# Scores of an HGRN2 head for both directions in one call: wide products first, then 24 narrow ones on four column groups

## The chip, the cores and the metric

The kernel runs on one core of one Trainium2 chip. The metric is the device time of one execution in microseconds. Three runs of the kernel before gave 887.88, 888.44 and 889.48 us; the median, 888.44, is the time before.

## What is computed

The reference runs two blocks of a network over 256 latent tokens (and 256 context tokens) of width 1024. The change is in the first block's mixer, a gated linear recurrence with 8 heads (HGRN2), done in both directions and in chunks of 64 tokens:

```python
b = jnp.cumsum(logf, axis=3)                      # within a chunk of 64
qe = q * jnp.exp(b - b_ref); ke = k * jnp.exp(b_ref - b)
scores = jnp.where(mask, jnp.einsum('bhnik,bhnjk->bhnij', qe, ke), 0.0)
o_intra = jnp.einsum('bhnij,bhnjv->bhniv', scores, v)
...
o_inter = jnp.einsum('bhnik,bhnkv->bhniv', q * jnp.exp(b), s_start)
```

For each head and direction the outputs are masked scores times values, plus the queries times the state at the chunk's start. The results of the two directions are added, normalized per head, multiplied by a gate and multiplied by an output matrix. Ahead of all this stands a modulation (shift, scale and gate vectors of a product with `w_ada`), whose parts are summed over partitions by small products.

## The kernel before, in words

All weights are streamed: SyncE loads halves of a chunk (128 x 1024) into a ring of eight raw buffers, ScalarE makes the high part (`hi`, line 154) and VectorE the low part (`lo`, line 155) of each, and a projection multiplies in three products per k tile (lines 355 to 357: high by high, high by low, low by high). The order of the work on each engine is the order in which the program is written; nothing is rescheduled.

The HGRN2 part takes the heads in four pairs p = 0 to 3. For each pair there are projections for the forget gates of the two directions (`ff`, `fb`), for `q` and for `v`; `gates(d)` (VectorE and ScalarE) makes the factors `qe`, `ke`, `Q`, `K` and `kc` of a direction. `hg_side` then gives the pair's small products as a list of steps:

- `T_(hh)`: transposes of `kc` (line 618), copied to `kcT` by ScalarE (line 620).
- `SC_(hh, d)`: the scores of one head and direction in one PSUM bank. In each of the two blocks of 128 tokens, the two chunks' diagonal parts are done with 32 stationary columns (lines 640 and 642, 64 and 32 moving tokens); then one 128x128 product between the blocks (line 645); then two products between the chunks of a block with 64 stationary columns (line 651). VectorE copies the diagonal parts under a mask into `sct` (line 657), ScalarE copies the rest (lines 659 and 664), and with the second direction VectorE adds the two directions into `scm` (line 662).
- `S_(hh)`: the state (line 626), read from `kcT`. `O_(hh)`: the output (line 684) and its normalization (lines 689 to 692). `OT_(hh)`: transposes of the result (line 698).

A float32 product is two passes in the trace, each with its own weight load: 64 calls of line 640 give 128 loads and 128 matmuls. All of these steps take banks from a ring of four, named `x`; a step waits until the readers of the bank's last use are done.

The steps of pairs 0 to 2 stand in the list `side`; `fm_product` and the second `fb` loop call `tick` after each four k tiles, which puts one or two steps into TensorE's queue. The steps of pair 3 have no projections of a next pair to go among, and go by the list `slots` among the four products of the output gate (`g`, p = 0 to 3), one slot after each four k tiles, twelve passes. `ada_flush` puts the two sums over partitions of a part of the modulation (`ada_rows`, lines 592 and 593; each takes one bank `x`) behind the gate product p = 1. After the gate products, `row_product` multiplies by the output matrix.

Of the kernel before, what the change touches and what calls it, by code (L numbers as in the profile page):

```python
# [9 lines left out]
F32 = mybir.dt.float32  # L10
# [6 lines left out]
D = 1024  # L17
# [33 lines left out]
def kernel(ctx: ExitStack, tc: tile.TileContext, a, out):  # L51
# [17 lines left out]
    # A chunk is one or two halves of up to 1024 columns. A half is loaded, then split exactly into two  # L69
    # float32r parts, hi + lo.  # L70
    halves, chunks = [], []

    def add(hs, kind="split"):
        """hs: per half (parts, k tiles, columns); a part is (view of the half's tile, source)."""
        first = len(halves)
        for parts, k, n in hs:
            halves.append((parts, k, n, kind))
            assert k * n <= 1024, (k, n)
        chunks.append((first, len(halves)))
        return len(chunks) - 1  # L80
# [19 lines left out]
    class SplitPool:  # L100
        """Buffers for the two parts of bufs halves, for the halves under limit."""
# [13 lines left out]
    def pump(limit, hold=False):  # L115
        """Issue the loads and the splits that have a free buffer, splits of halves under limit only."""
# [49 lines left out]
    def use(i, keep=None, ahead=None):  # L166
        """The k tiles of chunk i as a list of (hi, lo); chunks before it (or before keep) are done with."""
# [17 lines left out]
    def part_done(i):  # L185
        """The first half of chunk i is done with."""
# [137 lines left out]
    def rstd_of(ms, width=1, n=1):  # L324
        """(ms / n + eps) ^ -0.5; ms [128, width], or [128, 2] to be added."""
# [8 lines left out]
    def mean_sq(junk, x, ms):  # L334
        """ms = the part of the mean over D of x ^ 2 that x holds."""
# [44 lines left out]
    def fm_product(chunk, nk=KT, x=None, tag="x", ticks=0):  # L380
        """Two feature tiles of a product over lat tokens -> one bank [128, 2, T]."""
# [65 lines left out]
    # rstd of the tokens, then the same on every partition  # L447
# [44 lines left out]
    # products of the gates, with the sums (a), the features (s) and the next weights' splits among them  # L492
# [66 lines left out]
    def ada_step(parts=(3, 4, 2)):  # L559
        """One chunk of the rest of the modulation: sums over k on each partition, then over partitions."""  # L560
# [49 lines left out]
    def hg_side(p, el, vt):  # L610
# [20 lines left out]
        def SC_(hh, d):  # L631
            e = el[d]
            z = bank("x")
            zd = z[:, 0:256].rearrange("p (b t) -> p b t", b=2)
            ha, hb = (0, 32) if d == 0 else (32, 0)
            for b in range(2):
                for c in range(2):
                    o = hh * 256 + b * 128 + 64 * c
                    ra, rb = slice(64 * c + ha, 64 * c + ha + 32), slice(64 * c + hb, 64 * c + hb + 32)
                    t_.matmul(zd[ra, b, 64 * c:64 * c + 64], e["ke"][:, o + ha:o + ha + 32], e["qe"][:, o:o + 64],  # L640
                              start=True, stop=True)
                    t_.matmul(zd[rb, b, rb], e["ke"][:, o + hb:o + hb + 32], e["qe"][:, o + hb:o + hb + 32],
                              start=True, stop=True)
            b1, b2 = e["blk"]
            t_.matmul(z[:, 256:384], flat(e["K"][:, hh, b1, e["k"], :]), flat(e["Q"][:, hh, b2, e["c"], :]),
                      start=True, stop=True)
            rA = slice(0, 64) if d == 0 else slice(64, 128)
            cB = slice(64, 128) if d == 0 else slice(0, 64)
            zo = z[:, 384:512].rearrange("p (b t) -> p b t", b=2)
# [846 lines left out]
```

## Time and profile before

| | us |
|---|---|
| median of the runs (lowest, highest) | 888.44 (887.88, 889.48) |
| span of the profiled execution, first to last instruction | 886.7 |
| TensorE matmul busy | 863.0 (97%) |
| TensorE weight load busy | 781.0 (88%) |
| VectorE busy | 618.6 (70%) |
| ScalarE busy | 512.9 (58%) |

The profile is of one execution, and only its span is given; a run's time has in addition what lies around the span, and the median of the runs is 1.7 us above it. In a row of a timeline the first number is the start in us from the span's start, the second the length in us, then come engine, line, instruction, `out<-in` with shapes, and how many instructions are merged in the row. The length of a matmul's record holds its way through the array, so records overlap, and the pace of TensorE is read from start to start.

### The profile page before, as it was taken

What the parts mean: (1) busy time and instruction counts of PE and PEld (TensorE: products, weight loads), DVE (VectorE), ACT (ScalarE), POOL (GpSimd) and SP (SyncE); (2) the same over time, 40 slices, a digit from 0 to 9 for tenths busy, and PEclk for the clock granted to TensorE, in tenths of its full rate; (3) what the DMA queues carried; (4) which work ended last, traced back from release to release, by engine and by line L of the source; (5) the groups of instructions that cost most, each with busy time, mean ns of one, the idle gap of its engine ahead of it and who ended that gap; (6) DMA issues with size and microseconds to landing.
All of it is one profiled execution on the core that took longest, in us unless ns stands there. A gap on an engine that the chain in (4) does not pass through costs nothing.

```text
span 886.7 us, 15396 instructions
## 1 busy us (share of the span) xinstructions
PE 863.0 (97%) x6144; PEld 781.0 (88%) x6144; DVE 618.6 (70%) x955; ACT 512.9 (58%) x823; POOL 17.3 (2%) x27
## 2 busy tenths in 40 slices
PE   4999999999999999999999999999999999999997
PEld 2679897988978999999998799999999899999995
DVE  7876878776888778977767736766486587555532
ACT  6877575673857575655545745756463575444431
POOL 1000000000000000000000000000000000000000
PEclk9999999999999999999999999999999999999999
DMA  9984472733634458776764374445596087656401
GB/s 313 276 280 167 131 250 78 258 116 116 216 122 156 154 192 294 253 246 208 236 213 95 122 225 138 130 141 158 184 312 195 24 285 243 191 190 190 161 1 47
DMA packets 131967, 161.98 MB, mean 183 GB/s; under 512 B 14136, under 2 KB 114488, under 8 KB 131896
## 3 DMA queue, kind: packets, MB, share of 16 engines
q1 hardware_dynamic: 129728, 155.80, 55.0%
q10 hardware_dynamic: 2168, 5.20, 1.7%
q8 instruction: 48, 0.79, 0.3%
q14 instruction: 23, 0.19, 0.1%
HBM read 159.93 MB, written 1.05 MB: 182 GB/s over the span
## 4 chain that ended last, share of the span: by engine, by line
PE 91%; ACT 3%; DVE 3%; DMA 2%; issue 1%; POOL 0%; SPq 0%; POOLq 0%; DVEq 0%; ACTq 0%
PE m L355 17%; PE m L356 17%; PE m L357 17%; PE x L355 8%; PE x L357 8%; PE x L356 8%; PE x L684 2%; DMA xT<-in_xcT_dram 1%; PE m L345 1%; PE x L345 1%; PE m L346 1%; PE m L341 1%; PE x L626 1%; PE x L346 1%; DMA raw<-in_hg_w_in_dram 1%; PE x L341 1%
## 5 line engine op out<-in xcount | busy, mean ns | idle before, releaser
L155 DVE TENSOR_TENSOR lo<-raw,hi 128x1024 fp32r<-128x1024 f32 (+1 forms) x264 | 310.0, 1204 | 134.0 <-ACT hi L154 131.0
L154 ACT ACTIVATE hi<-raw 128x1024 fp32r<-128x1024 f32 (+1 forms) x264 | 265.7, 1038 | 121.1 <-PE x L356 51.0
L355 PE MATMUL m<-hTh,hi 128*128 128x256 f32 (+1 forms) x560 | 178.8, 319 | 0.6 <-ACT hTh L425 0.6
L356 PE MATMUL m<-hTl,hi 128*128 128x256 f32 (+1 forms) x560 | 171.7, 307 | 0.2 <-DVE hTl L432 0.2
L357 PE MATMUL m<-hTh,lo 128*128 128x256 f32 (+1 forms) x560 | 171.4, 306 | 0.0
L355 PE MATMUL x<-hTh,hi 128*128 128x256 f32 x592 | 166.2, 281 | 0.0
L356 PE MATMUL x<-hTl,hi 128*128 128x256 f32 x592 | 165.1, 279 | 0.0
L357 PE MATMUL x<-hTh,lo 128*128 128x256 f32 x592 | 165.1, 279 | 0.0
L355 PEld LDWEIGHTS m<-hTh,hi 128*128 128x128 f32 x560 | 105.8, 189 | 9.2 <-issue 2.9
L355 PEld LDWEIGHTS x<-hTh,hi 128*128 128x128 f32 x592 | 111.2, 188 | 1.0 <-ACT hi L154 0.2
L356 PEld LDWEIGHTS x<-hTl,hi 128*128 128x128 f32 x592 | 110.8, 187 | 1.0 <-issue 0.2
L357 PEld LDWEIGHTS x<-hTh,lo 128*128 128x128 f32 x592 | 111.2, 188 | 0.0
L356 PEld LDWEIGHTS m<-hTl,hi 128*128 128x128 f32 x560 | 105.8, 189 | 5.7 <-DVE hTl L432 0.8
L357 PEld LDWEIGHTS m<-hTh,lo 128*128 128x128 f32 x560 | 105.4, 188 | 5.8 <-DVE lo L155 0.4
L355 PE MATMUL m<-hi,ah 128*128 128x512 f32 x248 | 97.2, 392 | 0.0
L357 PE MATMUL m<-hi,al 128*128 128x512 f32 x248 | 96.8, 391 | 0.0
L356 PE MATMUL m<-lo,ah 128*128 128x512 f32 x248 | 96.5, 389 | 0.0
L357 PEld LDWEIGHTS m<-hi,al 128*128 128x128 f32 x248 | 46.5, 188 | 10.6 <-DVE al L1141 0.4
L356 PEld LDWEIGHTS m<-lo,ah 128*128 128x128 f32 x248 | 46.6, 188 | 8.9
L355 PEld LDWEIGHTS m<-hi,ah 128*128 128x128 f32 x248 | 46.6, 188 | 8.9 <-ACT ah L1137 0.2
L355 PE MATMUL m<-hi,hTh 128*128 128x256 f32 x128 | 36.2, 283 | 0.0
L575 DVE SCALAR_TENSOR_TENSOR vr<-raw,cs,vr 128x1024 f32<-128x1024 f32 x28 | 35.8, 1280 | 0.4
(302 smaller groups left out, 1267.4 us busy)
## 6 DMA issues: line engine op xcount, KB each, us to landing
raw<-in_ffn_w_up_dram SPq DMA_DIRECT2D x44, 512.0 KB, 5.7
raw<-in_w_in_dram SPq DMA_DIRECT2D x42, 512.0 KB, 3.6
raw<-in_hg_w_in_dram SPq DMA_DIRECT2D x36, 512.0 KB, 4.9
raw<-in_w_ada_dram SPq DMA_DIRECT2D x32, 512.0 KB, 4.9
raw<-in_w_up_dram SPq DMA_DIRECT2D x32, 512.0 KB, 4.7
raw<-in_w_down_dram SPq DMA_DIRECT2D x32, 512.0 KB, 3.6
raw<-in_ffn_w_down_dram SPq DMA_DIRECT2D x22, 512.0 KB, 4.5
raw<-in_w_ada_dram SPq DMA_DIRECT2D x32, 256.0 KB, 4.5
```

Source lines behind the costliest of these rows:

```text
L154: s_.activation(h[:, :w], r[:, :w], AF.Copy)
L155: held.append(lambda r=r, h=h, l=l, w=w: v_.tensor_tensor(l[:, :w], r[:, :w], h[:, :w].bitcast(F32), op=OP.subtract))
L341: t_.matmul(o, hTl[:, k, c], w[k][0], start=False, stop=k == KT - 1)
L345: t_.matmul(o, hTh[:, k, c], w[k][0], start=k == 0, stop=False)
L346: t_.matmul(o, hTh[:, k, c], w[k][1], start=False, stop=False)
L355: t_.matmul(o, wh, xh, start=start, stop=False)
L356: t_.matmul(o, wh, xl, start=False, stop=False)
L357: t_.matmul(o, wl, xh, start=False, stop=stop)
L575: v_.scalar_tensor_tensor(acc, w[kk][0], cs[:, k:k + 1], acc, op0=OP.mult, op1=OP.add)
L626: t_.matmul(z[:, d * 128:(d + 1) * 128], kcT[hh][:, (2 * d + j) * 128:(2 * d + j + 1) * 128], vt[:, j, hh * 128:(hh + 1) * 128], start=j = ...
L684: t_.matmul(z[:, b * 128:(b + 1) * 128], l, r, start=i == 0, stop=i == len(terms) - 1)
```

## The change

`SC_` is called once per head and does both directions in two banks. First come the two 128x128 products between the blocks. The products between chunks, with 64 stationary columns before, are split into two of 32. All 24 products with 32 columns are put on lists by the 32-column group (PSUM partitions 0, 32, 64, 96) they write, six per group, and issued in rounds over the four groups. Copies and sums come behind all of them. The list of steps keeps its length by two empty steps (`len`). For the last pair the slots are set anew: the scores of both heads stand in the last two slots of gate product 2, the states in the first two, the outputs one slot later than before. `ada_flush` stands behind gate product 2 instead of 1. Comments and docstrings removed elsewhere are left out here.

```diff
             St[hh] = wk.tile([128, 2, 128], F32, tag="St", name="St")
             s_.activation(flat(St[hh]), z[:, 0:256], AF.Copy)
 
-        def SC_(hh, d):
-            e = el[d]
-            z = bank("x")
-            zd = z[:, 0:256].rearrange("p (b t) -> p b t", b=2)
-            ha, hb = (0, 32) if d == 0 else (32, 0)
-            for b in range(2):
+        def SC_(hh):
+
+
+
+            zs, groups = [], [[] for _ in range(4)]
+            for d in range(2):
+                e = el[d]
+                z = bank("x")
+                zs.append(z)
+                b1, b2 = e["blk"]
+                t_.matmul(z[:, 256:384], flat(e["K"][:, hh, b1, e["k"], :]), flat(e["Q"][:, hh, b2, e["c"], :]),
+                          start=True, stop=True)
+                zd = z[:, 0:256].rearrange("p (b t) -> p b t", b=2)
+                zo = z[:, 384:512].rearrange("p (b t) -> p b t", b=2)
+                ha, hb = (0, 32) if d == 0 else (32, 0)
+                for b in range(2):
+                    for i in range(2):
+                        g = 2 * d + i
+                        groups[g].append((zo[32 * g:32 * g + 32, b, :], e["K"][:, hh, b, e["sA"], 32 * i:32 * i + 32],
+                                          e["Q"][:, hh, b, e["sB"], :]))
+                    for c in range(2):
+                        o = hh * 256 + b * 128 + 64 * c
+                        ga, gb_ = 2 * c + ha // 32, 2 * c + hb // 32
+                        rb = slice(32 * gb_, 32 * gb_ + 32)
+                        groups[ga].append((zd[32 * ga:32 * ga + 32, b, 64 * c:64 * c + 64],
+                                           e["ke"][:, o + ha:o + ha + 32], e["qe"][:, o:o + 64]))
+                        groups[gb_].append((zd[rb, b, rb], e["ke"][:, o + hb:o + hb + 32],
+                                            e["qe"][:, o + hb:o + hb + 32]))
+            for n in range(max(len(g) for g in groups)):
+                for g in groups:
+                    if n < len(g):
+                        t_.matmul(*g[n], start=True, stop=True)
+            for d in range(2):
+                z, sc = zs[d], sc_t[d, hh]
+                zd = z[:, 0:256].rearrange("p (b t) -> p b t", b=2)
+                zo = z[:, 384:512].rearrange("p (b t) -> p b t", b=2)
+                ha, hb = (0, 32) if d == 0 else (32, 0)
+                rA = slice(0, 64) if d == 0 else slice(64, 128)
+                cB = slice(64, 128) if d == 0 else slice(0, 64)
                 for c in range(2):
-                    o = hh * 256 + b * 128 + 64 * c
-                    ra, rb = slice(64 * c + ha, 64 * c + ha + 32), slice(64 * c + hb, 64 * c + hb + 32)
-                    t_.matmul(zd[ra, b, 64 * c:64 * c + 64], e["ke"][:, o + ha:o + ha + 32], e["qe"][:, o:o + 64],
-                              start=True, stop=True)
-                    t_.matmul(zd[rb, b, rb], e["ke"][:, o + hb:o + hb + 32], e["qe"][:, o + hb:o + hb + 32],
-                              start=True, stop=True)
-            b1, b2 = e["blk"]
-            t_.matmul(z[:, 256:384], flat(e["K"][:, hh, b1, e["k"], :]), flat(e["Q"][:, hh, b2, e["c"], :]),
-                      start=True, stop=True)
-            rA = slice(0, 64) if d == 0 else slice(64, 128)
-            cB = slice(64, 128) if d == 0 else slice(0, 64)
-            zo = z[:, 384:512].rearrange("p (b t) -> p b t", b=2)
-            for b in range(2):
-                t_.matmul(zo[rA, b, :], e["K"][:, hh, b, e["sA"], :], e["Q"][:, hh, b, e["sB"], :],
-                          start=True, stop=True)
-            sc = sc_t[d, hh]
-            for c in range(2):
-                for r, q_ in ((slice(64 * c, 64 * c + 64), hb), (slice(64 * c + ha, 64 * c + ha + 32), ha)):
-                    i = slice(64 * c + q_, 64 * c + q_ + 32)
-                    v_.copy_predicated(sc[r, :, i], hmask[r, d:d + 1, i].to_broadcast([r.stop - r.start, 2, 32]),
-                                       zd[r, :, i])
-            s_.activation(sc[rA, :, cB], zo[rA], AF.Copy)
-            if True and d:
-                scm[hh] = wk.tile([128, 2, 128], F32, tag="scm", name="scm", bufs=2)
-                v_.tensor_add(scm[hh], sc_t[0, hh], sc)
-            xS[hh, d] = wk.tile([128, 128], F32, tag="xs", name="xs", bufs=4)
-            s_.activation(xS[hh, d], z[:, 256:384], AF.Copy)
+                    for r, q_ in ((slice(64 * c, 64 * c + 64), hb), (slice(64 * c + ha, 64 * c + ha + 32), ha)):
+                        i = slice(64 * c + q_, 64 * c + q_ + 32)
+                        v_.copy_predicated(sc[r, :, i], hmask[r, d:d + 1, i].to_broadcast([r.stop - r.start, 2, 32]),
+                                           zd[r, :, i])
+                s_.activation(sc[rA, :, cB], zo[rA], AF.Copy)
+                xS[hh, d] = wk.tile([128, 128], F32, tag="xs", name="xs", bufs=4)
+                s_.activation(xS[hh, d], z[:, 256:384], AF.Copy)
+            scm[hh] = wk.tile([128, 2, 128], F32, tag="scm", name="scm", bufs=2)
+            v_.tensor_add(scm[hh], sc_t[0, hh], sc_t[1, hh])
 
         def O_(hh):
             z = bank("x")
...
                     b1, b2 = e["blk"]
                     ql = flat(e["Q"][:, hh, b, e["c"], :]) if b == b1 else e["q2"][:, hh, :]
                     terms.append((ql, St[hh][:, d, :]))
-                    if hh in scm:
-                        if d:
-                            terms.append((scm[hh][:, b, :], vt[:, 2 + b, hc]))
-                    else:
-                        terms.append((sc_t[d, hh][:, b, :], vt[:, 2 + b, hc]))
+                    if d:
+                        terms.append((scm[hh][:, b, :], vt[:, 2 + b, hc]))
                     if b == b2:
                         terms.append((xS[hh, d], vt[:, 2 + b1, hc]))
                 for i, (l, r) in enumerate(terms):
...
                 t_.transpose(z[:, b * 128:(b + 1) * 128], on[hh][:, b * 128:(b + 1) * 128], ident)
             s_.activation(oT[p][:, hh, :], z[:, 0:256], AF.Identity, scale=vec("gn"))
 
-        order = [(T_, 0), (T_, 1), (SC_, 0, 0), (SC_, 0, 1), (SC_, 1, 0), (SC_, 1, 1), (S_, 0), (S_, 1),
-                 (O_, 0), (O_, 1)]
+        order = [(T_, 0), (T_, 1), (SC_, 0), (len, ()), (SC_, 1), (len, ()), (S_, 0), (S_, 1), (O_, 0), (O_, 1)]
         late = [(OT_, 0), (OT_, 1)]
         return tuple([lambda f=f: f[0](*f[1:]) for f in x] for x in (order, late))
 
...
-    T0, T1, SC00, SC01, SC10, SC11, S0, S1, O0, O1 = work
+    T0, T1, SC0, _, SC1, _, S0, S1, O0, O1 = work
     OT0, OT1 = late
-    slots = [[], [[T0], [T1], [], [SC00]], [[S0], [SC10, S1], [SC01], [SC11]], [[O0], [O1], [], [OT0]]]
+    slots = [[], [[T0], [T1], [], []], [[S0], [S1], [SC0], [SC1]], [[], [O0], [O1], [OT0]]]
...
-        if p == 1:
+        if p == 2:
             ada_flush()
```

## Rows read from the trace of the kernel before

**Rows 1.** The head of the profile page: span, then busy us, share and instructions.
```profile
span 886.7 us, 15396 instructions
PE 863.0 (97%) x6144; PEld 781.0 (88%) x6144; DVE 618.6 (70%) x955; ACT 512.9 (58%) x823; POOL 17.3 (2%) x27
```

**Rows 2.** What TensorE waited for, whole span: us in total, times, longest.
```profile
PE x L466 <- DVE sq L456: 11.8, 1, 11.8
PE x L592 <- ACT kcT L620: 1.8, 1, 1.8
PE x L345 <- DVE hTh L989: 1.0, 2, 0.8
```

**Rows 3.** Stretches: us, busy of PE, PEld, DVE, ACT, POOL, granted clock, DMA.
```profile
250.62:254.60 3.98, 3.98 (x14) 2.95 (x15) 3.98 (x6) 1.38 (x2) 0.00 (x0) 0.57 0.32 115
...
96.00:130.00 34.00, 34.00 (x315) 31.16 (x314) 26.49 (x52) 20.18 (x40) 1.40 (x2) 1.00 0.67 218
```

**Rows 4.** Timeline of TensorE around the two score calls of head 0.
```profile
96.25 0.39 PE L356 MATMUL m<-hTl,hi 128*128 128x512 f32 x1
96.47 0.40 PE L357 MATMUL m<-hTh,lo 128*128 128x512 f32 x1
96.80 0.24 PE L640 MATMUL x<-qe,ke 128*32 128x64 f32 x1
96.81 0.22 PE L642 MATMUL x<-qe,ke 128*32 128x32 f32 x1
...
96.88 0.22 PE L640 MATMUL x<-qe,ke 128*32 128x64 f32 x1
...
96.94 0.22 PE L640 MATMUL x<-qe,ke 128*32 128x64 f32 x1
96.94 0.20 PE L642 MATMUL x<-qe,ke 128*32 128x32 f32 x1
...
97.16 0.49 PE L645 MATMUL x<-Q,K 128*128 128x128 f32 x2
...
99.10 0.50 PE L355 MATMUL m<-hTh,hi 128*128 128x512 f32 x1
```

**Rows 5.** Timeline of TensorE, output products of head 0.
```profile
110.43 0.39 PE L684 MATMUL x<-St,Q 128*128 128x128 f32 x2
110.65 0.39 PE L684 MATMUL x<-St,q 128*128 128x128 f32 x2
```

**Rows 6.** Timeline of VectorE: last factor of pair 0, and idle time before splits.
```profile
96.70 0.41 DVE L829 TENSOR_TENSOR K<-K,b 128x256 f32<-128x256 f32 x1
...
111.06 2.36 DVE L155 TENSOR_TENSOR lo<-raw,hi 128x1024 fp32r<-128x1024 f32 x2 [1.06 <-ACT hi L154]
...
215.60 2.36 DVE L155 TENSOR_TENSOR lo<-raw,hi 128x1024 fp32r<-128x1024 f32 x2 [2.30 <-ACT hi L154]
```

**Rows 7.** Timeline of TensorE around the end of gate product 1.
```profile
246.36 0.28 PE L357 MATMUL m<-hTh,lo 128*128 128x256 f32 x1
...
247.72 1.12 PE L592 MATMUL x<-vr,ones 128*128 128x512 f32 x2
250.62 1.88 PE L592 MATMUL x<-vr,ones 128*128 128x512 f32 x2 [1.78 <-ACT kcT L620]
...
254.60 1.06 PE L626 MATMUL x<-vt,kcT 128*128 128x128 f32 x8
```

**Rows 8.** Timelines of ScalarE and VectorE in the same stretch.
```profile
249.98 1.08 ACT L620 ACTIVATE kcT<-x 128x512 f32<-128x512 f32 x2
...
250.88 1.22 DVE L155 TENSOR_TENSOR lo<-raw,hi 128x1024 fp32r<-128x1024 f32 x1
```

**Rows 9.** Timelines of TensorE and VectorE, head 7's output to the last transposes.
```profile
270.98 0.36 PE L355 MATMUL m<-hTh,hi 128*128 128x256 f32 x1
...
272.96 0.61 DVE L692 TENSOR_SCALAR on<-x,r 128x128 f32<-128x128 f32 x2 [0.88 <-POOL r L322]
273.89 0.60 PE L698 MATMUL x<-ident,on 128*128 128x128 f32 x4
```

## Prediction

> **What bounds the kernel now.** I read the head of the profile page first: TensorE is busy for 863.0 of 886.7 us [rows 1]. Busy records of matmuls overlap, so the next view is the list of what TensorE waited for. There, 11.8 us at the very start and 1.8 us on line 592 are the only waits above 1 us [rows 2]. The table of stretches then shows that in the HGRN2 part VectorE is busy for 26.49 of 34 us and ScalarE for 20.18, while DMA moves at 0.67 of its share [rows 3]. So TensorE's queue is the path, and an edit is worth the TensorE time it takes away, as long as VectorE, at three quarters of the time, can follow. The last view is the timeline of TensorE around one pair of score calls [rows 4], around the last pair of heads [rows 7] and at the end of the gate products [rows 9].
>
> **The scores of pairs 0 to 2 (six heads).** Each float32 product is two passes. In one head, TensorE goes from the last pass of a projection (96.47) to the next projection's first pass (99.10). A projection pass is followed by the next after 0.22 to 0.23 us (96.25 to 96.47), so the score work proper starts at 96.70 and takes 2.40 us. It is two calls, each with three kinds of stationary width: 32, 128, 64. At each change of width nothing is in flight for a moment: from 96.47 the 0.23 of the pass itself would end at 96.70, and the first 32-column pass starts at 96.80. That is 0.10 us per change. The 32-column part of one call lasts from 96.80 to the first 128-column pass at 97.16, 0.36 us [rows 4].
>
> The new call, step by step. First two 128x128 products, one for each direction: four passes at 0.11 us (two passes from 110.43 to 110.65 [rows 5]), 0.44 us; they have the width of the projection before them, so no change is paid there. Then one change, 0.10. Then 24 products with 32 columns, 48 passes, 12 on each 32-column group: eight of 64 tokens and four of 32. The 64-token passes of one group follow each other at about 0.06 us (96.88 to 96.94). The 32-token passes of two groups, eight of them, start between 96.81 and 96.94, at a pitch of about 0.04 within a group. That these start between the starts of the 64-token ones shows that the four groups run side by side. So a group needs 8 x 0.06 + 4 x 0.04 = 0.64 us. Behind the last pass comes what the old part shows behind its own four 64-token passes, 0.36 - 4 x 0.06 = 0.12. Sum: 0.44 + 0.10 + 0.64 + 0.12 = 1.30 us instead of 2.40, a gain of 1.10 per head. Bounds for the 0.64: at best a group never waits at all and its 32-token passes take half of a 64-token one (0.60); if the rounds of four march in step, 12 x 0.06 = 0.72; with no overlap of groups at all, 32 x 0.06 + 16 x 0.04 = 2.56.
>
> Of these heads, the first has a new wait. Its call now needs both directions' factors at once. The last write to K for the second direction ends on VectorE at 96.70 + 0.41 = 97.11 [rows 6]; the second 128x128 product would start at 96.70 + 0.22 = 96.92. That costs 0.2 us once. In the other pairs, the same factor is ready before the call. Six heads: 6 x 1.10 - 0.2 = 6.4 us.
>
> Queues behind this: the mask copies and ScalarE's copies keep their number and their order by direction; the sum of the two directions comes as before behind both. The second bank is asked for 1.2 us earlier than before, and it is one whose reader (the copy of transposed factors) comes a projection half earlier, so I cost that at nothing; without that cover it would be some tenths of a microsecond per call. VectorE has to follow a TensorE that is 2.2 us earlier per pair. It last stood idle before splitting weights for 1.06 us in pair 0 and 2.30 in pair 2 [rows 6], so in pair 0 it may come up to 1.1 us late on the splits; these are for the product after next, so I take nothing for it.
>
> The Trainium skill speaks against many small passes: "TensorE: Matmul & The Clock Gate", section "Wait — 56ns, not 53.3ns?", says that starts of matmuls never come closer than about 25 ns, and about 62 ns where the sequencer's software decodes them. By 62 ns the 48 passes would take 3.0 us and the call 3.6, longer than the old 2.40. Here the trace disagrees: passes of different column groups start at 96.80 and 96.81 [rows 4].
>
> **The last pair (heads 6 and 7).** Its products stand among the gate products. Four calls go, each 247.72 - 246.48 = 1.24 us (246.36 plus one 0.12 pass to line 592 [rows 7]) plus 0.10 for the change back, 5.4 us; two calls of 1.30 + 0.10 come, 2.8 us: 2.6 gained. Against it stand the waits. Before: the first call and the modulation's two sums (line 592) stood at the end of gate product 1; the second sum waited 1.78 us for ScalarE's copy of transposed factors, which had held its bank, until 250.62, and after that the granted clock averaged 0.57 for 3.98 us, so most of it lay at the lower of the two levels, 1.2 GHz [rows 3, 7]; that is 3.98 x 0.43 = 1.7 us lost. Both have moved behind gate product 2. But that copy, on ScalarE from 249.98 [rows 8], is not moved by the edit, since ScalarE has a full queue ahead of it, and the state product of head 6 (before at 254.60 [rows 7]) reads that very copy. What is late next: gate product 2 now starts at 246.5, does its first twelve passes of 0.12 in 1.4 us, and stands from 247.9 to 250.6: 2.7 us instead of 1.8. The low part of the weights behind it is ready at 250.88 + 1.22 = 252.1 [rows 8], when the state product is just done at the lower clock, so that adds nothing. I take the clock's loss behind the wait as the same 1.7. So 0.9 is lost.
>
> A second loss at the end: the output products of the last head move one slot later, so that only twelve gate passes (1.4 us) and one transpose (0.2) stand between them and the transposes that read their result. Before, the gate product went on at 270.98 and the normalized rows were written at 272.96 + 0.61 = 273.57 [rows 9], that is 2.6 us, where there were 2.9 us of work. Now 1.6: a wait of 1.0 us. The two sums of the modulation behind gate product 2 take two banks, those of the head called one slot before; its second copy comes about when the bank is asked for, 0 to 0.5, I take 0.3. Sum for the last pair: 2.6 - 0.9 - 1.0 - 0.3 = +0.4 us.
>
> Both parts: 6.8 us off the path. Behind the HGRN2 part TensorE waits for nothing longer than a microsecond [rows 2], so the lead is carried to the end. The profiled execution then has a span of 886.7 - 6.8 = 879.9; the shown median is 888.44, 1.7 above that span, and so I forecast 881.6.
>
> **The rivals.**
> (a) VectorE doesn't follow. For it: 26.49 of 34 us busy, and only 1.06 us idle at its tightest place [rows 3, 6]. Against it: it idles for 2.30 in pair 2, so it starts each pair level. If the pairs keep just the slack shown (1.06, and 1.7 each as a middle value for two more), 4.5 of the 6.4 are kept, and with 1.0 more lost at the last pair: 888.44 - 3.9 = 884.5.
> (b) The last pair goes worse: the longer wait brings a second stretch at the lower clock (1.7 more, as the first cost), and a further 0.9 at a bank. 888.44 - 6.8 + 2.6 = 884.2. The 1.0 us wait at the end is shorter than the 1.78 after which the clock fell, which speaks against it.
> (c) The wait of the last pair goes: ScalarE gets to its copy earlier, so that both 2.7 and 1.7 vanish: 881.6 - 4.4 = 877.2. Against it: ScalarE has no gap before 249.98 that TensorE could give back.
> (d) Slower: the column groups don't overlap when two banks and two directions are mixed. The place is the 32-column part; its price is 2.56 instead of 0.64, so a call costs 3.22 against 2.40, 0.82 lost in each of six heads (4.9), and in the last pair 2 x 3.32 against 5.4 with 2.2 of waits (3.4): 888.44 + 8.3 = 896.7. It decides from 0.64 + 1.10 = 1.74 us for that part on. For it only that no mixture of banks is in the old trace; against it the starts 0.01 us apart. The Trainium skill's 62 ns floor, told above, would end near this case.
> (e) TensorE's gain is all given back at the next limit, and nothing is measured: 888.
>
> **How the numbers follow.** Forecast 0.52, (a) 0.18, (b) 0.12, (c) 0.08, (d) 0.05, (e) 0.05. The forecast's own bounds: 0.72 instead of 0.64 costs 8 x 0.08 = 0.6, the clock's loss can differ by 1.7 either way: 879.5 to 883.5. With (a) and (b) the range that leaves out 2 in 10 is 878.4 to 885.4. A change of under 0.2% (1.8 us) can't be told from none. Faster: forecast, (a), (b) and (c), less 0.02 of their tail, 0.88; no change: (e) and that tail, 0.07; slower: (d), 0.05.
>
> **What would show it.** The score lines' 64-column products are gone; from the first 128x128 product to the next projection pass 1.2 to 1.4 us per head, with 48 short passes in 0.6 to 0.75; pair 0 shows a wait of some 0.2 for K. From the start of gate product 0 on everything lies 6 to 6.5 us earlier. A wait on the state product for ScalarE's copy of 2 to 3 us replaces that on line 592, with one stretch of lower clock behind it; about 1 us of wait before the last transposes. The forecast is wrong if the short passes take over 1 us, if gate product 0 starts less than 5 us earlier, or if the last pair gains or loses over 2 us.

## The result: 882.1 us against 888.2

The changed kernel took 882.1 us (median of four runs, 881.8 to 882.48), the kernel before 888.16 beside it (887.13 to 889.48): a ratio of 0.9929, 95% interval 0.9913 to 0.9945 (estimated from the single executions, so it can differ by up to 0.001 from the quotient of two medians). In a later series the same two gave 881.19 and 888.04, 0.9921 [0.9908, 0.9935]. The forecast was 881.6 with a range of 878.4 to 885.4. One execution of one variant below (e11) took 1058.43 us at a mean granted clock of 0.755; it counts in that variant's median and not in its ratio.

The head of the profile after, and what TensorE waited for (the columns are those of [rows 1] and [rows 2]):

```profile
span 880.2 us, 15524 instructions
PE 854.1 (97%) x6208; PEld 778.0 (88%) x6208; DVE 618.1 (70%) x955; ACT 513.0 (58%) x823; POOL 17.2 (2%) x27
```

```profile
PE x L466 <- DVE sq L456: 11.5, 1, 11.5
PE x L626 <- ACT kcT L620: 2.9, 1, 2.9
...
PE x L710 <- DVE on L704: 0.5, 1, 0.5
```

There are 64 more matmul records (each of the eight heads has eight more) and TensorE is still busy for 97% of the span. The wait for ScalarE's kcT has moved from line 592 [rows 2] to the state product on line 626 and grown from 1.8 to 2.9 us.

Where the time went is read from landmarks that both kernels share: the first transposes of kc in each pair of heads (line 618) and the first pass of the output matrix (tile yh). Timeline of TensorE, first the kernel before, then after:

```profile
93.07 0.38 PE L618 MATMUL x<-ident,kc 128*128 128x128 f32 x2
...
145.34 0.27 PE L618 MATMUL x<-ident,kc 128*128 128x128 f32 x1
...
197.62 0.38 PE L618 MATMUL x<-ident,kc 128*128 128x128 f32 x2
...
241.41 0.27 PE L618 MATMUL x<-ident,kc 128*128 128x128 f32 x1
...
274.24 0.48 PE L355 MATMUL m<-hi,yh 128*128 128x512 f32 x1
```

```profile
94.25 0.38 PE L618 MATMUL x<-ident,kc 128*128 128x128 f32 x2
...
144.61 0.38 PE L618 MATMUL x<-ident,kc 128*128 128x128 f32 x2
...
194.44 0.38 PE L618 MATMUL x<-ident,kc 128*128 128x128 f32 x2
...
235.53 0.38 PE L618 MATMUL x<-ident,kc 128*128 128x128 f32 x2
...
267.78 0.48 PE L355 MATMUL m<-hi,yh 128*128 128x512 f32 x1
```

From one landmark to the next, after against before: pair 0 50.36 against 52.27 (-1.91), pair 1 49.83 against 52.28 (-2.45), pair 2 41.09 against 43.79 (-2.70), last pair 32.25 against 32.83 (-0.58); together -7.64. Behind the last landmark the span goes on for 612.5 us in one and 612.4 in the other. Ahead of the first one, where the two kernels issue the same work in the same order, the profile after is 1.18 us longer. That makes 6.5, the difference of the spans. The 1.18 is looked at below, under e7. At the transposes of the last pair, twelve passes into gate product 1, TensorE is 5.88 us earlier in the changed kernel (235.53 against 241.41), and 7.06 if both are counted from the first landmark; the prediction had 6 to 6.5 from gate product 0 on.

One score call after (head 1, timeline of TensorE):

```profile
102.12 0.39 PE L357 MATMUL m<-hTh,lo 128*128 128x512 f32 x1
102.35 0.60 PE L641 MATMUL x<-Q,K 128*128 128x128 f32 x4
102.89 0.25 PE L662 MATMUL x<-Q,K 128*32 128x64 f32 x2
...
103.61 0.51 PE L355 MATMUL m<-hTh,hi 128*128 128x512 f32 x1
```

From the last projection pass (102.12) to the next (103.61) it takes 1.49 us where the two old calls took 99.10 - 96.47 = 2.63 [rows 4]. The two 128-wide products and the change of width take 0.54, the 48 narrow passes with the change back 0.72.

In head 0 one more wait shows, in a longer record of the same line; VectorE's last write to K stands beside it (timelines of TensorE and VectorE):

```profile
97.89 0.95 PE L641 MATMUL x<-Q,K 128*128 128x128 f32 x4
98.77 0.25 PE L662 MATMUL x<-Q,K 128*32 128x64 f32 x2
```

```profile
97.88 0.42 DVE L840 TENSOR_TENSOR K<-K,b 128x256 f32<-128x256 f32 x1
```

The narrow products start 0.88 us behind the wide ones and not 0.54. The other 0.34 us are read as waiting for K, which is complete at 98.30.

The last pair after, in the timelines of ScalarE and TensorE, and in the table of stretches (columns as in [rows 3]):

```profile
244.53 1.08 ACT L620 ACTIVATE kcT<-x 128x512 f32<-128x512 f32 x2
```

```profile
245.17 1.92 PE L626 MATMUL x<-vt,kcT 128*128 128x128 f32 x8 [2.95 <-ACT kcT L620]
...
249.15 1.05 PE L626 MATMUL x<-vt,kcT 128*128 128x128 f32 x8
...
267.43 0.59 PE L710 MATMUL x<-ident,on 128*128 128x128 f32 x2 [0.51 <-DVE on L704]
```

```profile
245.17:249.00 3.83, 3.83 (x19) 3.83 (x20) 3.83 (x6) 3.59 (x6) 0.00 (x0) 0.55 0.31 80
```

kcT is copied 9.0 us behind the transposes (244.53 - 235.53; before 249.98 - 241.41 = 8.6 [rows 8]), TensorE stands for 2.95 us, and behind that the granted clock averages 0.55 over 3.83 us: most of that stretch lies at the lower of its two levels, 1.2 GHz instead of 2.4.

### The profile page after: what moved, and what is told of

It is laid out like the page before. It is cut to its first block, busy times and chain, and to the rows that moved or that the text cites. A ratio compares the mean times of both kernels' runs of the same rounds, so it can differ in the third digit from the quotient of the medians.

```text
span 880.2 us, 15524 instructions
## 1 busy us (share of the span) xinstructions
PE 854.1 (97%) x6208; PEld 778.0 (88%) x6208; DVE 618.1 (70%) x955; ACT 513.0 (58%) x823; POOL 17.2 (2%) x27
## 4 chain that ended last, share of the span: by engine, by line
PE 87%; DVE 5%; ACT 5%; issue 1%; DMA 1%; POOL 0%; POOLq 0%; DVEq 0%; ACTq 0%
PE m L355 16%; PE m L356 16%; PE m L357 16%; PE x L355 8%; PE x L357 8%; PE x L356 8%; PE x L696 2%; DVE lo L155 1%; PE x L626 1%; ACT hi L154 1%; PE m L345 1%; PE x L345 1%; PE m L346 1%; PE m L341 1%; PE x L346 1%
```

## The experiments

The table has each kernel's median, its ratio to the kernel before in the same series, and two numbers of its profiled execution: where the first transposes of pair 0 start, and the rest of the span from there. The rest is the better measure of an edit: the first part has the same work in all of them and differs by up to 5 us.

| kernel | median us | ratio [95%] | first transposes | rest of the span |
|---|---|---|---|---|
| before | 888.16 | | 93.07 | 793.6 |
| after | 882.1 | 0.9929 [0.9913, 0.9945] | 94.25 | 785.9 |
| after again (e7) | 881.19 | 0.9921 [0.9908, 0.9935] | 95.37 | 786.2 |
| e1 order only | 889.53 | 1.0014 [1.0002, 1.0025] | 91.25 | 794.8 |
| e2 sums early | 879.38 | 0.9912 [0.989, 0.9933] | 95.92 | 786.4 |
| e3 group by group | 890.58 | 1.0029 [1.0018, 1.0039] | 94.48 | 797.1 |
| e4 three widths | 881.28 | 0.993 [0.991, 0.9949] | 91.99 | 786.7 |
| e5 transposes earlier | 880.63 | 0.9919 [0.9901, 0.9937] | 94.33 | 787.2 |
| e6 one direction | 883.8 | 0.9954 [0.994, 0.9967] | 91.18 | 789.2 |
| e8 both moves | 880.99 | 0.9928 [0.9906, 0.9949] | 96.01 | 786.2 |
| e9 scores sooner | 879.11 | 0.9899 [0.9881, 0.9916] | 90.87 | 785.8 |
| e10 GpSimd | 881.82 | 0.9933 [0.9912, 0.9953] | 92.12 | 787.6 |
| e11 all moves | 881.46 | 0.9929 [0.9903, 0.9954] | 94.67 | 785.1 |

**e1: the order alone.** The old score calls in the changed kernel's slots, with its later modulation sums.

```
-    slots = [..., [[T0], [T1], [], [SC00]], [[S0], [SC10, S1], [SC01], [SC11]], [[O0], [O1], [], [OT0]]]
+    slots = [..., [[T0], [T1], [], []], [[S0], [S1], [SC00, SC01], [SC10, SC11]], [[], [O0], [O1], [OT0]]]
-        if p == 1:
+        if p == 2:
             ada_flush()
```

> The kernel before, with its old score calls (one per direction, three widths), but with the new slots of the last pair and the modulation's sums behind gate product 2. Theory (the gain is all in the score calls; the new order costs): the last pair loses about 1.2 us at the wait for ScalarE's copy of transposed factors (2.9 instead of 1.8) and 0.5 at the last transposes, and saves 0.3 by two calls standing together: 0.5 to 2 us slower than the kernel before, so 888.7 to 890.2 beside a kernel before at 888.2. Rival (the new order is where a part of the gain comes from): faster than the kernel before by 1 us or more, 887 or less.

TensorE's wait in e1 (a second one, of 0.5 us, stands at the last transposes):

```profile
PE x L626 <- ACT kcT L620: 2.6, 1, 2.6
```

It is slower than before by 1.2 us in the rest of the span and by 0.14% in the ratio. So the new order alone costs time, 1.2 us where the prediction's three terms had 0.9 + 1.0 + 0.3, and the whole gain is in the new calls.

**e3: the same products, one column group after the other.**

```
-            for n in range(max(len(g) for g in groups)):
-                for g in groups:
-                    if n < len(g):
-                        t_.matmul(*g[n], start=True, stop=True)
+            for g in groups:
+                for x in g:
+                    t_.matmul(*x, start=True, stop=True)
```

> The changed kernel with the same 24 narrow products in another order: all six of the first column group, then all of the second, and so on, instead of rounds over the four groups. Theory A (groups overlap only if neighbours in the queue belong to different groups): the narrow part takes about 4 x 0.64 = 2.6 us instead of 0.64, 1.9 us more in each of eight heads, some 15 us: 895 to 898. Theory B (the queue finds the other groups' products by itself, however they are ordered): no change, 881.5 to 883. In between, the queue looks ahead for a part of a group.

Timeline of TensorE, head 2 of e3:

```profile
150.97 0.60 PE L641 MATMUL x<-Q,K 128*128 128x128 f32 x4
151.50 0.30 PE L661 MATMUL x<-Q,K 128*32 128x64 f32 x2
...
153.47 0.50 PE L355 MATMUL m<-hTh,hi 128*128 128x512 f32 x1
```

The narrow part takes 1.97 us instead of 0.72: 1.25 per head, and the kernel is slower than the one before. The 1.97 holds the change of width behind the last pass, for which the prediction had 0.12; with it the prediction's two bounds are 2.68 with no overlap and 0.76 with all of it, and the time lies between them. By these two estimates something over a third of the overlap is left when the products are issued group by group ((2.68 - 1.97) / (2.68 - 0.76) = 0.37). The gain hangs on the round robin order, not on the use of four groups alone. Eight heads at 1.25 make 10.0 of the 11.2 us by which the rest of the span is longer than in the changed kernel; in the last pair of e3 TensorE also stays at the lower clock for longer (0.50 over the 6 us from 252.89, where its wait for kcT ends).

**e4: three widths again.** The blocks of 64 columns are kept as they were, between the wide and the 32-column products.

```
-                    for i in range(2):
-                        g = 2 * d + i
-                        groups[g].append((zo[32 * g:32 * g + 32, b, :], e["K"][:, hh, b, e["sA"], 32 * i:32 * i + 32],
-                                          e["Q"][:, hh, b, e["sB"], :]))
+                    wide.append((zo[64 * d:64 * d + 64, b, :], e["K"][:, hh, b, e["sA"], :],
+                                 e["Q"][:, hh, b, e["sB"], :]))
...
+            for i in (0, 2, 1, 3):
+                t_.matmul(*wide[i], start=True, stop=True)
```

> The changed kernel with the products between chunks left at 64 stationary columns, as in the kernel before: two products of 128, then four of 64, then sixteen of 32, both directions together. Theory (a change of width costs 0.10 before and about 0.12 behind its last pass, the passes themselves run at 0.06 per 64 tokens and group): per head 0.44 + 0.10 + 0.23 + 0.12 + 0.10 + 0.40 + 0.12 = 1.51 instead of 1.26, 0.2 to 0.3 more in each of eight heads: 883.5 to 884.7 beside 882.1. Rival (splitting the 64-column products is what fills the groups and is worth most of the gain): 886 or more. Rival (the width change is free when both directions share it): 882 to 882.7.

Timeline of TensorE, head 1 of e4:

```profile
100.71 0.40 PE L357 MATMUL m<-hTh,lo 128*128 128x512 f32 x1
100.95 0.61 PE L641 MATMUL x<-Q,K 128*128 128x128 f32 x4
101.48 0.45 PE L658 MATMUL x<-Q,K 128*64 128x64 f32 x8
...
102.36 0.50 PE L355 MATMUL m<-hTh,hi 128*128 128x512 f32 x1
```

1.65 us per head instead of 1.49. So merging the 64-column blocks into the narrow groups is worth 0.16 of the 1.14 us per head, and the rest comes from the order and from taking both directions together. Eight times 0.16 is 1.3 us, and the run time doesn't show it: the median of 881.28 lies below all that the expectation allowed, and its ratio can't be told from the changed kernel's. In the profile the rest of the span is 0.8 us longer than after; e4's has no stretch at the lower clock behind its wait of 2.57 us for kcT, which covers a part of the loss.

**e6: one direction per call.** The old kernel in its old order, each call with the new widths: its 128-wide product first, then twelve 32-column products round robin.

```
-            for b in range(2):
-                for c in range(2):
...
             t_.matmul(z[:, 256:384], flat(e["K"][:, hh, b1, e["k"], :]), flat(e["Q"][:, hh, b2, e["c"], :]),
...
+            groups = [[] for _ in range(4)]
             for b in range(2):
-                t_.matmul(zo[rA, b, :], e["K"][:, hh, b, e["sA"], :], e["Q"][:, hh, b, e["sB"], :],
-                          start=True, stop=True)
+                for i in range(2):
+                    g = 2 * d + i
...
+            for n in range(max(len(g) for g in groups)):
+                for g in groups:
+                    if n < len(g):
+                        t_.matmul(*g[n], start=True, stop=True)
```

> The kernel before with one edit: inside each score call (still one direction per call, same order, same place of the modulation sums) the 128-wide product is issued first and the 64-column ones are split into 32-column groups and issued round robin with the others. Theory A (the gain is the change of widths and its switches; calling both directions together adds little): a direction takes 0.10 + 0.22 + 0.36 + 0.12 = 0.8 instead of 1.30 us, so about 1.0 per head of pairs 0 to 2 is gained against 1.13 in the changed kernel, and the last pair, whose order is untouched, gains 1.5 to 2 more: median 880 to 881.5, no slower than the changed kernel. Theory B (the pairing of directions is what fills the groups evenly): half the gain or less, 883.5 to 885.5.

Timeline of TensorE, head 3 of e6:

```profile
150.85 0.38 PE L637 MATMUL x<-Q,K 128*128 128x128 f32 x2
151.16 0.25 PE L659 MATMUL x<-Q,K 128*32 128x64 f32 x2
...
151.73 0.49 PE L637 MATMUL x<-Q,K 128*128 128x128 f32 x2
...
152.73 0.50 PE L355 MATMUL m<-hTh,hi 128*128 128x512 f32 x1
```

A direction takes 0.88 to 1.0 us, not the 0.8 of theory A. From its first product to the next projection a head takes 1.88, in the changed kernel 1.26 (102.35 to 103.61), before 2.30 (96.80 to 99.10). So of this part of the gain 0.4 comes from the widths and their order and 0.6 from taking both directions together; theory B is the nearer one. The narrow products of one direction cost 0.57 (151.16 to 151.73) and those of both 0.72: a call pays its change of width back once, whatever it holds, and one direction fills the groups unevenly, with four products on two of them and two on the others.

**e2, e5, e8 to e11: the last pair.** These take the changed kernel and move its work in the last pair. The edits, each against the changed kernel:

```
 e2:  -        if p == 2:          +        if p == 1:            # ada_flush(), the modulation sums
 e5:  - [[], [[T0], [T1], [], []], ...   + [[[], [], [T0], [T1]], [[], [], [], []], ...
 e8:  e5 and e2
 e9:  e2 and  - [[S0], [S1], [SC0], [SC1]], [[], [O0], [O1], [OT0]]
              + [[S0], [SC0], [SC1], [S1]], [[O0], [O1], [], [OT0]]
 e10: e5 and  + x_ = nc.gpsimd if p == 3 else v_     # for the two passes on lines 838 and 840
 e11: e5, e2, e9 and e10
```

> The changed kernel with one line put back: the modulation's sums stand behind gate product 1 again; the new slots stay. Theory (TensorE stands 2.9 us at the state product and then runs 3.4 us at the lower clock only because nothing stands ahead of it that does not need ScalarE's copy; the sums now find banks that nobody holds, since no score call stands ahead of them): the wait falls under 0.5 us, the stretch at 1.2 GHz behind it goes, and the time is 3 to 4.5 us below the changed kernel, 877.6 to 879 beside 882.1. Rival A (the sums' second bank waits for the same copy as in the kernel before): a wait of 1 us or more stands at line 592 and the time is within 1 us of the changed kernel. Rival B (the time at the lower clock is not tied to the wait): the wait goes, the stretch stays, 879.5 to 880.5.

TensorE's waits in e2:

```profile
PE x L710 <- DVE on L704: 2.2, 1, 2.2
...
PE x L626 <- ACT kcT L620: 1.2, 1, 1.2
```

The sums' work ahead of the state products shortens the wait for kcT by 1.7 us, as far as it goes. But TensorE is then at the last transposes sooner than VectorE's norm, and 2.2 us of wait stand there, with a clock of 0.57 from 268.70 to 272.70, behind it. The rest of the span is no shorter than the changed kernel's. None of the expectation's three cases came: the wait for kcT fell to 1.2 and not under 0.5, and the lower clock went with the wait to another place.

> The changed kernel with one edit: in the last pair the transposes of k (T0, T1) stand in the third and fourth slot of the product before (g of pair 0) and not in the first two of g of pair 1; the same work otherwise. Theory A (the 2.9 us wait ahead of the state products is ScalarE's order: the copies to kcT stand behind the Silu table load, a Silu and a weight split, all of them issued before the transposes): the copies now stand ahead of the table load and end about 2.7 us earlier, the wait of 2.9 falls below 0.5, and the stretch at the lower clock behind it (1.7 us of extra time) goes too; TensorE's time from the transposes of the last pair to the output matrix falls by 2.9 to 4.6 us against the changed kernel, the median lies at 877.5 to 879.5. Theory B (VectorE ends last in the last pair, so that TensorE being earlier only meets a later wait, at the last output products or the last transposes): 2 us or more come back there, the median stays at 880 to 882.

ScalarE, VectorE and TensorE in e5:

```profile
241.55 1.05 ACT L620 ACTIVATE kcT<-x 128x512 f32<-128x512 f32 x2
```

```profile
245.30 1.22 DVE L155 TENSOR_TENSOR lo<-raw,hi 128x1024 fp32r<-128x1024 f32 x1
```

```profile
246.57 0.58 PE L357 MATMUL m<-hTh,lo 128*128 128x256 f32 x1 [3.00 <-DVE lo L155]
...
248.87 1.91 PE L626 MATMUL x<-vt,kcT 128*128 128x128 f32 x8
```

```profile
246.57:251.82 5.25, 5.25 (x24) 5.25 (x25) 5.16 (x6) 2.55 (x5) 0.00 (x0) 0.50 0.73 201
```

kcT now comes in time, and the wait for it is gone. In its place TensorE waits 3.00 us for the low part of the next weights, which VectorE splits only when it is done with both directions' factors (245.30), and the clock behind it averages 0.50 over 5.25 us, a stretch 1.4 us longer than the one in the profile after. The state product of the second head starts at 248.87, in the profile after at 249.15: 0.3 us are left of the 2.9. By the output matrix even these are gone: from the transposes of pair 2 to there e5 takes 74.72 us (194.31 to 269.03), the profile after 73.34. Theory A was right about ScalarE's order and wrong about its worth: the split was due at nearly the same time, and the wait that the profile names was only the first in the queue. Theory B had the time (880 to 882) and VectorE as the reason, but looked for the wait at the last products and not at the split.

> The changed kernel as it is, once more, beside the others on the same chip. Both theories: median 881.5 to 882.6. For the start-up part (start to the first transposes of the first pair: 93.07 us in the profile before, 94.25 in the one after): if the 1.18 us between them belong to the change they are seen again, above 94; if they are chance of the execution it can lie anywhere from 91 to 96.

The repeat of the changed kernel gave 881.19 us. Its start-up part is again above 94 (95.37), as in e2, e3, e5, e8 and e11, while e4, e9 and e10, which begin with the same work, have 91.99, 90.87 and 92.12. So the 1.18 us are no fixed price of the change. What divides the long from the short is in the traces: in all seven above 94 TensorE waits 1.1 to 1.5 us for the first tokens, and its granted clock from 23.5 to 27 us is 0.50 to 0.62; in the other six, the kernel before, e1 and e6 among them, that wait is 0.6 at most and the clock 1.00. Why the wait is longer in some executions was not found. Whether long start-ups come more often with the change (7 of 10 profiles of the changed kernel and its variants, none of three of the old one and e1 and e6) stays open too. In e2, e3, e5, e7 and e8 the profiled execution is the longest of its kernel, so the profiles count too many; but the mean granted clock of a whole execution is 0.995 or below in 7 of 10 executions of the changed kernel, and in 6 of 45 of the kernel before in the later series. That speaks for it, though the mean doesn't say where in an execution the clock was low.

> e5 with the modulation sums of the last pair before its state products instead of behind its scores (where the kernel before had them). Theory A: no wait for kcT in either place, the sums only change which VectorE work lies ahead of the last norm: 877 to 879, within 1 us of e5. Theory B (VectorE late in the last pair): with the sums gone from between scores and output products, the output products wait for the score sums or the last transposes wait 2 us or more, and a stretch at the lower clock behind it: 879 to 881.

In e8 TensorE waits 2.2 us at the last transposes and 1.5 for the split: both waits that e2 and e5 brought are there, the second at half its size. Theory B.

> The kernel of e2 (the changed one with the modulation sums of the last pair ahead of its state products) with the slots of the last pair moved too: scores in the second and third slot, the second head's state product behind them, the output products one slot sooner. Theory A (the 2.2 us ahead of the last transposes in e2 is only the place of the second output product, whose norm then has one free slot of 1.4 us too few): that wait falls below 0.8 and no stretch at the lower clock stands behind it, last pair 1.4 to 2.9 us shorter than in e2's profile (31.15 from its transposes to the output matrix, and 1.5 behind), median 877 to 879. Theory B (VectorE is full in the last pair): copies of scores that come sooner push the weight splits back, and TensorE waits for a split or for the score sums by 1.5 to 3 us instead: 879 to 881.

TensorE's waits in e9:

```profile
PE x L626 <- ACT kcT L620: 1.2, 1, 1.2
PE x L710 <- DVE on L704: 1.1, 1, 1.1
...
PE x L641 <- ACT St L629: 0.8, 1, 0.8
...
PE x L641 <- DVE K L840: 0.8, 1, 0.8
```

The wait at the last transposes halves, and a new one of 0.8 for a bank (ScalarE's copy of the state) takes part of it. That wait stands ahead of the second direction in the first score call. With no wait above 1.3 us in the last pair no stretch at the lower clock follows. This is the fastest kernel of the study by its median, 879.11 us. That it beats the changed kernel is likely but not shown: the intervals (0.9881 to 0.9916 and 0.9908 to 0.9935) overlap, and the rest of its span is the same within 0.1 us as that of the profile after. Two differences hide in that: from the transposes of pair 2 to the end e9 takes 684.98 us and the profile after 685.76, so 0.8 are gained at the last pair, and pair 0 takes 51.04 instead of 50.36, with a wait of 0.8 for K in head 0 that is 0.34 there. The wait at the last transposes stayed above the 0.8 of theory A.

> e5 (transposes of k one group sooner) with four passes of VectorE in the last pair, Q and K of the middle part in both directions (0.42 us each, 0.34 from start to start), given to GpSimd, which has nothing else there. Theory B (since e5: VectorE ends last, its split of the weights stands behind the gates' passes): the split comes 4 x 0.34 = 1.4 us sooner and the wait of 3.0 us in e5 falls to about 1.6, the run by 1 to 1.5 us against e5. Theory A (the wait of e5 is set by the weight's load or ScalarE's half of the split, VectorE only by appearance): the wait stays at 3.0 and the run the same as e5's. If GpSimd is much slower at these passes (over 1.5 us each) or slows VectorE down, the scores or the split come later, and it is slower than e5.

VectorE and GpSimd in e10 (one line of code was added, so its lines behind 837 are one higher):

```profile
238.39 0.58 DVE L847 TENSOR_TENSOR EE<-b 128x2 f32<-128x2 f32 x1
239.08 0.73 DVE L850 TENSOR_SCALAR q<-Q,EE 128x128 f32<-128x128 f32 x2
```

```profile
238.00 0.95 POOL L839 TENSOR_TENSOR Q<-Q,b 128x256 f32<-128x256 f32 x1 [21.53 <-DVE Q L833]
238.92 0.62 POOL L841 TENSOR_TENSOR K<-K,b 128x256 f32<-128x256 f32 x1
```

TensorE's wait for the split is 3.2 us. It is the third case of the expectation, GpSimd slowing VectorE down, rather than either theory: GpSimd takes two passes per direction away, and VectorE is no sooner for it. From the start of K's pass on line 834 to the next direction's qe it took 1.95 us here (237.79 to 239.74) and 1.86 in e5 (239.77 to 241.63), because the two small passes that stayed took 0.58 and 0.73 instead of 0.15 and 0.48. So this run doesn't say what a relieved VectorE would give; e5's reading of the split's place in VectorE's queue stands on the two starts alone (245.30 and 246.57).

> All the moves together: transposes of k sooner (e5), modulation sums ahead of the state products (e2), scores and output products sooner (e9), four passes on GpSimd (e10). Theory: the waits of the last pair for kcT (2.9 in the changed kernel), for the split (1.5 in e8) and for the last transposes (2.2 in e8) all fall below 1, and so does the time at the lower clock: from the transposes of the pair before it to the output matrix 69 to 71 us instead of 73.3, median 876.5 to 878.5. If VectorE's work only collides elsewhere, 879 to 881.

TensorE's waits in e11:

```profile
PE x L641 <- DVE vr L593: 1.9, 1, 1.9
PE m L357 <- DVE lo L155: 1.7, 1, 1.7
```

The waits for kcT and at the last transposes are gone, and two others stand in their places: the first score call wants for its second direction the bank that VectorE has still to read for the modulation sums, and the split is late as in e8. From the transposes of pair 2 to the output matrix it takes 72.46 us (194.65 to 267.11), not the 69 to 71 of the theory; the profile after has 73.34. The rest of the span, 785.1, is 0.8 below the profile after; the median (881.46, and 881.18 without the one long execution) is no better.

## Why the prediction was right, step by step

- **The new score call** was put at 0.44 + 0.10 + 0.64 + 0.12 = 1.30 us and measures 0.54 + 0.72 = 1.26; the gain per head is 1.14 instead of 1.10. e3 shows that the overlap of the groups, on which the 0.64 rested, is real and needs the round robin. Rival (d), no overlap, came part of the way in e3: a call takes 0.54 + 1.97 = 2.51 there, against its 3.22. So its mechanism exists and sits in the order of issue.
- **The wait for K in head 0**: 0.2 forecast, 0.34 measured. It was 0.8 in e9 and e4, which came to their first transposes 3.4 and 2.3 us earlier than the profile after, but 0.35 in e10, 2.1 us earlier; so an early TensorE doesn't settle it alone, and what does was not found.
- **VectorE follows** (rival a): pairs 1 and 2 gained 2.45 and 2.70, at least the 2.28 of their score calls. The 0.2 and 0.4 beyond it lie spread over the projection passes of 256 tokens, which follow each other a little faster (in pair 2, 199 steps take 23.24 us instead of 23.66); e6 has the 0.4 of pair 2 too, e1 and e4 don't. Its cause was not found.
- **The wait for kcT**: 2.7 instead of 1.8 forecast, 2.95 measured, with about the same stretch at the lower clock behind it (0.55 over 3.83 us, before 0.57 over 3.98 [rows 3]). The forecast's 2.7 counts from the start of one product to the next and the 1.8 only idle time; idle time alone went from 1.78 to 2.95, so 1.2 were lost where 0.9 stood in the sum. That this price belongs to the order and not to the calls is shown by e1.
- **The wait at the last transposes**: 1.0 forecast, 0.5 measured. **The bank of the modulation sums**: 0.3 forecast, none seen. The last pair was to gain 0.4 and gained 0.6. With the 2.6 of its calls and the waits as measured it would have gained 0.9; where the other 0.3 went was not traced.
- **The forecast of the total** came out 0.5 below the first median and 0.4 above the second. The sum was off by 0.9 (7.7 instead of 6.8 us in the rest of the span), and the start-up of the profiled execution, taken as unchanged, hid it by being 1.18 longer. That the total came out so near is thus in part luck. The forecast's own bounds don't follow from their terms either: 0.6 and 1.7 above 881.6 make 883.9 and not 883.5, and 1.7 below it makes 879.9 and not 879.5; nothing hung on it.
- **Rival (c)**, the last pair's wait going, was refused because ScalarE has no gap ahead of its copy. e5 brought the copy forward by issuing it sooner, and a wait of 3.0 us stayed: the stronger reason is VectorE's split, which the prediction had at 252.1 and took to cost nothing, since it was hidden behind the wait for the copy and the state product at the lower clock. In the changed kernel it was hidden there indeed; in e5, with the copy out of the way, it wasn't.

## What to carry to other kernels

Where small products with few stationary columns are many, gather them by width, issue the wide ones beside their like, and deal the narrow ones out over the column groups in turn; each call pays its changes of width and its unfilled groups once, so here two half calls joined were worth more than the change of widths (0.6 against 0.4 us per head). Before moving the work that a wait is put down to, look for what else would be ready only then: in the last pair the copy and the split were due within 2 us of each other, a bank and the norm came next, and six rearrangements moved the wait about, with a gain of 0.8 us at best in a profile and none that the run times can tell for sure.

## What the runs showed of the hardware

**Column groups and the order of issue.** 24 narrow products take 0.72 us dealt out over four groups, 15 ns for each of their 48 passes, and 1.97 issued group by group (e3). The two times together are read so: a product that waits for its group mostly holds up those behind it in the queue, for other groups too.

**GpSimd beside VectorE.** A pass of VectorE on 128x2 elements took 0.58 us instead of 0.15 while GpSimd multiplied (238.39 to 238.97; GpSimd's pass ended at 238.95). The Trainium skill, "SBUF — State Buffer", section "SBUF: two separate sides", says that the two engines share one pair of ports as an exclusive lock: of an operation of VectorE with two inputs from SBUF and an instruction of GpSimd that reads SBUF, the one that starts first has the pair for the whole of its instruction, and the other waits. The rows agree: GpSimd's pass began at 238.00, ahead of VectorE's two-input pass at 238.39, and that one ended 0.02 us behind it.

**The clock.** TensorE's granted clock fell to the lower level behind idle times of 2.95 (after), 2.58 (e1), 2.2 (e2) and 1.78 us [rows 7], but not behind 1.90 in e11, nor 1.68 in e6. The same 2.57 us at the same place had both outcomes, the lower level in e3 and none in e4, so the length of an idle time alone doesn't tell. Timeline of TensorE, e3 and then e4; the longer record is the one at the lower clock:

```profile
252.89 2.08 PE L626 MATMUL x<-vt,kcT 128*128 128x128 f32 x8 [2.57 <-ACT kcT L620]
```

```profile
244.74 1.16 PE L626 MATMUL x<-vt,kcT 128*128 128x128 f32 x8 [2.57 <-ACT kcT L620]
```

The table of stretches for 23.5 to 27 us, before and then after:

```profile
23.50:27.00 3.50, 3.50 (x21) 2.74 (x22) 3.00 (x5) 3.20 (x6) 0.00 (x0) 1.00 0.97 275
```

```profile
23.50:27.00 3.50, 3.50 (x10) 2.81 (x10) 3.34 (x6) 2.85 (x5) 0.00 (x0) 0.51 0.98 282
```

Ahead of it TensorE had waited 0.56 us for the first tokens in the one and 1.42 in the other. The work up to there is the same, and over the 13 profiles the first transposes start between 90.87 and 96.01. So a profile of one execution can carry up to 5 us that belong to no edit, and two profiles are compared from a landmark behind the start-up.
